# A row tile's partial products: three matmuls of 256 columns in place of one of 512 and one of 256, with packed operand rows

## The chip, the cores and the metric

The kernel runs on one core of a Trainium2 chip. The metric is the device time of one execution in microseconds. Matrix products run on TensorE (PE; PEld is its loading of the stationary operand), elementwise work on VectorE (DVE), ScalarE (ACT) and GpSimd (POOL), and the weights are brought in by transfers that SyncE (SP) issues.

## The reference, cut to what matters

One layer of a hybrid decoder on 256 tokens with 16 learned tokens ahead of them, width 2048, all in float32:

```python
def hybrid_mixer(xn, ...):
    proj = xn @ w_in
    (fq, fk, fv, ff, gq, gk, gv, gr, ga, gate_fox, gate_gla) = jnp.split(proj, split_points, axis=-1)
    o_fox = forgetting_attention(fq, fk, fv, ff, b_forget)        # 8 heads of 128
    ...
    o_gla = gated_linear_attention(gq, gk, gv, g_log)             # 4 heads, keys 256, values 512
    o_gla = (head_rmsnorm(o_gla, gla_norm_g) * jax.nn.silu(gr)).astype(xn.dtype)
    y = jax.nn.sigmoid(gate_fox) * (o_fox @ w_o_fox) + jax.nn.sigmoid(gate_gla) * (o_gla @ w_o_gla)
    return y @ w_out

def squared_relu_mlp(xn, w1, w2):
    return jnp.square(jax.nn.relu(xn @ w1)) @ w2

h = h + hybrid_mixer(rmsnorm(h, norm_mix_g[l]), ...)
h = h + squared_relu_mlp(rmsnorm(h, norm_mlp_g[l]), w_ff1[l], w_ff2[l])      # 2048 -> 8192 -> 2048
return rmsnorm(h, final_norm_g)[:, N_META:]
```

The weights, some 290 MB, are read once.

## The kernel before

Activations lie transposed: 128 features on the partitions, tokens along the row. Every float32 operand is split in two parts that TensorE takes in its rounded float32 form, `hi` and the remainder `lo`, and a product is made of three partial products: hi·hi, hi·lo and lo·hi. The weights are cut into 128-column blocks of 2048 rows (`stream()` lists them in order). `weight_half` loads half a block (128 x 1024, L118), ScalarE makes `whi` of it (L120) and VectorE `wlo` (L121); five buffers of each rotate.

`gemm2` multiplies one weight block with an operand of 256 tokens. It runs over 16 row tiles `k` (8 for the fox output projection). Per row tile `mac2` issues two matmuls: `hi` with the whole operand row of 512 columns (256 columns of hi, then 256 of lo) into a whole PSUM bank (L136), and `lo` with the 256 hi columns into the bank's first half (L137). So the first half of the bank collects hi·hi + lo·hi, and the second half hi·lo. Whoever takes the result out adds the halves: `total` copies the second half to SBUF on ScalarE (L168) and adds it on VectorE (L171), and `add_residual` does so with one more addition (L858 to L860). Three banks of the pool `pg` rotate.

Where the 16 learned tokens are needed too (keys and values of both branches), `gemm_all` issues three matmuls of 272 columns per row tile instead (L153 to L155) and `join` mends the first 16 columns.

The first seven blocks are multiplied while the input still arrives, two row tiles at a time, by `products` (L345, L350; one block with 272 columns at L347, L348 and L352). The last four blocks of the MLP (`ends`) go in two parts: lo·hi for 256 tokens (L912), then for each half of the tokens one matmul of two pieces of 128 columns, hi·hi and hi·lo (L928).

The operands: `x` (normalised input, rows of 544 words: 272 hi, 272 lo) for the input projection; `of`, `og` (outputs of the branches), `y` (their gated sum), `x2` (input of the MLP) and `a` (its hidden part, four groups `g` of 2048). The last five are made by `operand`, which gives each row tile 544 words, with 16 unused ahead of the 512 and 16 behind.

Order: GLA heads, fox heads, then per two output blocks four gates (`gate`), the fox and the GLA output projection; then the projection `w_out`, and per group 16 blocks of `w_ff1` and 16 of `w_ff2`. A scheduler orders each engine's instructions at build time; `later(n, fn)` puts a piece of work behind the n-th gemm from here, so that small matmuls stand between large ones. `gate` takes its bank with `total` and multiplies by the norm on POOL (L816).

Of the kernel before, what the change touches and what calls it, by code (L numbers as in the profile page):

```python
# [7 lines left out]
F32 = mybir.dt.float32  # L8
F32R = mybir.dt.float32r
# [3 lines left out]
ALU = mybir.AluOpType  # L13
# [3 lines left out]
P = 128  # L17
# [3 lines left out]
NT = 256  # L21
NA = NM + NT
EPS = 1e-6
FOX_H, FOX_D = 8, 128
# [41 lines left out]
def trunk(ctx: ExitStack, tc: tile.TileContext, hT, w_small, w_all, consts, w_alpha2, out):  # L66
    nc = tc.nc
    serial = [0]

    def nm(s):  # L70
        serial[0] += 1
        return f"{s}_{serial[0]}"

    const = ctx.enter_context(tc.tile_pool(name="const", bufs=1))
    keep = ctx.enter_context(tc.tile_pool(name="keep", bufs=1))
    wp = ctx.enter_context(tc.tile_pool(name="wp", bufs=5))
    tmp = ctx.enter_context(tc.tile_pool(name="tmp", bufs=2))
    dram = ctx.enter_context(tc.tile_pool(name="dram", bufs=1, space=bass.MemoryType.DRAM))
    pg = ctx.enter_context(tc.tile_pool(name="pg", bufs=3, space=PSUM))
# [4 lines left out]
    def bank(pool, s):  # L84
        return pool.tile([P, 512], F32, tag="bank", name=nm(s))
# [47 lines left out]
        return lambda k: (parts[k // HK][0][:, k % HK, :], parts[k // HK][1][:, k % HK, :])  # L133

    def mac2(ps, hi, lo, x, first, last):
        nc.tensor.matmul(ps, hi, x, start=first, stop=False)  # L136
        nc.tensor.matmul(ps[:, 0:NT], lo, x[:, 0, :], start=False, stop=last)  # L137

    def gemm2(w, x, k0=0, nk=KT):

        ps = bank(pg, "ps")
        for k in range(nk):
            hi, lo = w(k0 + k)
            mac2(ps, hi, lo, x[:, k], k == 0, k == nk - 1)
        issued()
        return ps
# [15 lines left out]
        nc.scalar.copy(b, ps[:, NA : NA + NM])  # L162
        nc.vector.tensor_tensor(ps[:, 0:NM], ps[:, 0:NM], b, op=ALU.add)

    def total(ps, t=None):

        b = tmp.tile([P, NT], F32, tag="evb", name=nm("evb"))
        nc.scalar.copy(b, ps[:, NT:512])  # L168
        if t is None:
            t = tmp.tile([P, NT], F32, tag="evt", name=nm("evt"), bufs=4)  # L170
        nc.vector.tensor_tensor(t, ps[:, 0:NT], b, op=ALU.add)  # L171
        return t

    def split_to(dst_hi, dst_lo, src):
# [42 lines left out]

    def operand(pool, name, nk=KT, at=0, **kw):


        row = 2 * NT + 32
        t = pool.tile([P, at + nk * row], F32R, name=nm(name), **kw)
        t = t[:, at:].rearrange("p (k r) -> p k r", r=row)
        return t[:, :, 16 : 16 + 2 * NT].rearrange("p k (o t) -> p k o t", t=NT)


    h = keep.tile([P, KT, NA + 3], F32, name="h")
# [88 lines left out]
    for s in range(KT // 2):  # L316
        if s + 3 < KT // 2:
            with tc.issue_after(load_stage(s + 3, 0).ins):
                load_h(nc.sync, 2 * s + 6, 2)
            last = load_stage(s + 3, 1).ins  # L320
        wa, wb = stages[s]
        for kk in range(2):
            k = 2 * s + kk
            nc.scalar.activation(x_hi[:, k], h[:, k, 0:NA], AF.Identity, scale=gain(0, k))
            nc.vector.scalar_tensor_tensor(x_lo[:, k, 0:NT], h[:, k, NM:NA], gain(0, k),
                                           x_hi[:, k, NM:].bitcast(F32), op0=ALU.mult, op1=ALU.subtract)
            xm = meta[:, k, :]
# [12 lines left out]

        def products(c, k, part):
            hi, lo = at[c][0][:, k % 2, :], at[c][1][:, k % 2, :]
            ps, st, sp = first_ps[c], k == 0, k == KT - 1
            if part == 0 and c < NF - 1:
                nc.tensor.matmul(ps, hi, x[:, k], start=st, stop=False)  # L345
            elif part == 0:
                nc.tensor.matmul(ps[:, 0:NA], hi, x_hi[:, k], start=st, stop=False)  # L347
                nc.tensor.matmul(ps[:, X_LO], hi, x_lo[:, k], start=False, stop=sp, skip_group_check=True)  # L348
            elif c < NF - 1:
                nc.tensor.matmul(ps[:, 0:NT], lo, x[:, k, 0], start=False, stop=sp)  # L350
            else:
                nc.tensor.matmul(ps[:, 0:NA], lo, x_hi[:, k], start=False, stop=sp)  # L352

        if s < KT // 2 - 1:
            groups = [range(4), range(4, NF)] if s else [range(2), range(2, 4), range(4, NF)]
            order = [(c, 2 * s + kk, part) for g in groups for kk in range(2) for part in range(2) for c in g]
        else:
            order = [(c, 2 * s + kk, part) for c in range(NF) for kk in range(2) for part in range(2)]  # L360
        for o in order:
            products(*o)
        if s in (3, 5, 6, 7):
            with tc.issue_after(copied):
                square((3, 5, 6, 7).index(s))
# [90 lines left out]
    og_box = []  # L456

    def og_tile():
        if not og_box:
            og_box.append(operand(keep, "og", tag="s2"))  # L460
        return og_box[0]

    def gla_gates(ts):
        sg = att.tile([P, 4, NT], F32, tag="sg", name=nm("sg"))
        for i in range(4):
            t = ts[i] if ts else total(gemm2(next_weights(), x))
            nc.vector.tensor_tensor(t, t, rbt, op=ALU.mult)
# [26 lines left out]
    def gla_head(hd, sg, ready=None):  # L494
# [25 lines left out]
            for i in range(2):  # L520
                keys(i, gemm_all(next_weights()))
        for i in range(2):
            t = ready[0][:, i, :] if ready else total(gemm2(next_weights(), x))
# [118 lines left out]
    att = cum.enter_context(tc.tile_pool(name="att", bufs=1, reuse_waits="tile"))  # L642

    join(first_ps[NF - 1])
    ts = [total(ps) for ps in first_ps[0:4]]
    qd0 = att.tile([P, 4, NT], F32, tag="so", name=nm("qd"))[:, 0:2, :]
    for i in range(2):
        total(first_ps[4 + i], qd0[:, i, :])
    ps = bank(pg, "psa")
    for k in range(KT):  # L650
        if k == HK:
# [53 lines left out]
    def fox_head(hd):  # L705
# [106 lines left out]


    def gate():
        t = total(gemm2(next_weights(), x))
# [10 lines left out]
    for j0 in range(0, KT, 2):  # L826
        gates = ahead if j0 == 0 else [gate() for _ in range(4)]
        w = next_weights()
        for j in range(2):
            t = total(gemm2(w, of, k0=8 * j, nk=8))  # L830
            nc.vector.tensor_tensor(gates[2 * j], gates[2 * j], t, op=ALU.mult)
        for j in range(2):
            t = total(gemm2(next_weights(), og))
            nc.vector.tensor_tensor(t, gates[2 * j + 1], t, op=ALU.mult)
# [8 lines left out]


    ht = h[:, :, NM:NA]
    x2 = operand(keep, "x2", tag="s2")

    def square_sum(j, acc):
        if j == 0:
# [4 lines left out]
            nc.gpsimd.tensor_tensor(acc, acc, sq, op=ALU.add)  # L854

    def add_residual(j, ps):
        b = tmp.tile([P, NT], F32, tag="evb", name=nm("evb"))
        nc.scalar.copy(b, ps[:, NT:512])  # L858
        nc.vector.tensor_tensor(ht[:, j, :], ps[:, 0:NT], ht[:, j, :], op=ALU.add)
        nc.vector.tensor_tensor(ht[:, j, :], ht[:, j, :], b, op=ALU.add)  # L860

    acc2 = gat.tile([P, NT], F32, tag="acc", name="acc2", bufs=1)
    for j in range(KT):
# [11 lines left out]


    def relu2(a, f, ps):
        t = total(ps)
        nc.vector.scalar_tensor_tensor(t, t, 0.0, r2b, op0=ALU.max, op1=ALU.mult)
        s = gat.tile([P, NT], F32, tag="asq", name=nm("asq"))  # L880
        nc.vector.tensor_tensor(s, t, t, op=ALU.mult)
        split_to(a[:, f, 0, :], a[:, f, 1, :], s)

    acc = gat.tile([P, NT], F32, tag="acc", name="acc3", bufs=1)
    for g in range(NG):
        a = operand(keep, "a", tag="s1")
        held = []
        for f in range(KT):
            ps = gemm2(next_weights(), x2)
# [169 lines left out]
```

## Time and profile before

| | us |
|---|---|
| median of 3 runs | 1596.99 |
| lowest and highest run | 1596.72, 1597.74 |
| span of the profiled execution, first to last instruction | 1595.0 |
| PE busy in it | 1585.0 |
| DVE busy | 1060.4 |
| ACT busy | 790.8 |
| POOL busy | 125.2 |

The profile is of one execution, whose span is 1595.0 us; what of an execution lies outside the span is read as the median less the span, 2.0 us. In the rows, `L136` is a line of the kernel, `ps<-x,whi` are the tiles written and read, `128x512` is partitions by columns, and of matmuls the durations overlap: the time that one takes from the next is the distance of their starts.

### The profile page before, as it was taken

Reading aid. Unit: us, or ns where it says so; the run is one execution under the profiler, and the core shown is the slowest. Engines: PE = TensorE matmul, PEld = TensorE weight load, DVE = VectorE, ACT = ScalarE, POOL = GpSimd, SP = SyncE. Lnnn points to the kernel's source line nnn. Section 1 sums busy time; section 2 is a strip of 40 time slices with the busy share of each in tenths; the row PEclk is TensorE's granted clock in tenths of the full one; section 3 lists DMA queues with packets and bytes.
Section 4 is the critical chain, followed back from the end, with each engine's and each line's share of the span. In section 5 each row is a group of like instructions: output and inputs, shape, how many; then the busy total and the mean of one; then the engine's idle time right before and its main releaser. Section 6 shows DMA issues by size and latency. Waiting matters only on the chain.

```text
span 1595.0 us, 25427 instructions
## 1 busy us (share of the span) xinstructions
PE 1585.0 (99%) x9812; PEld 1428.8 (90%) x9812; DVE 1060.4 (66%) x1659; ACT 790.8 (50%) x1271; POOL 125.2 (8%) x213
## 2 busy tenths in 40 slices
PE   9999999999999999999999999999999999999997
PEld 8999999999998888888888888888888888888887
DVE  7897757676655555555777776567655776567655
ACT  6665444454455444444555544444444444444563
POOL 6011000011100000000011000000000000000022
PEclk9999999999999999999999999999999999999999
DMA  9444545454445555555555555555555555555552
GB/s 323 156 164 155 180 157 183 167 188 164 159 167 181 191 186 189 189 191 187 186 195 186 188 193 187 188 191 190 187 190 190 186 189 193 186 188 193 186 183 97
DMA packets 86602, 293.09 MB, mean 184 GB/s; under 512 B 9112, under 2 KB 16800, under 8 KB 86352
## 3 DMA queue, kind: packets, MB, share of 16 engines
q1 hardware_dynamic: 85872, 289.62, 53.8%
q8 instruction: 77, 1.26, 0.3%
q0 software_dynamic: 176, 1.12, 0.2%
q10 hardware_dynamic: 432, 0.72, 0.1%
q14 instruction: 45, 0.37, 0.1%
HBM read 289.32 MB, written 2.11 MB: 183 GB/s over the span
## 4 chain that ended last, share of the span: by engine, by line
PE 99%; DMA 0%; issue 0%; POOL 0%; ACT 0%; DVE 0%; SPq 0%; POOLq 0%; ACTq 0%
PE ps L136 51%; PE ps L137 27%; PE psa L155 5%; PE psa L154 5%; PE psa L153 5%; PE ps L345 1%; PE ps L350 1%; PE ps L928 1%; PE pa L548 1%; PE ps L912 0%; DMA raw<-w_all_dram 0%; PE po L611 0%; POOL o L976 0%; PE po L188 0%; PE ps L348 0%
## 5 line engine op out<-in xcount | busy, mean ns | idle before, releaser
L121 DVE TENSOR_TENSOR wlo<-raw,whi 128x1024 fp32r<-128x1024 f32 x522 | 641.0, 1228 | 452.8 <-ACT whi L120 449.4
L120 ACT CAST whi<-raw 128x1024 fp32r<-128x1024 f32 x522 | 548.1, 1050 | 660.0 <-PE ps L136 493.1
L136 PE MATMUL ps<-x,whi 128*128 128x512 f32 x1952 | 683.8, 393 | 0.0
L137 PE MATMUL ps<-x,wlo 128*128 128x256 f32 x1952 | 548.5, 281 | 0.0
L136 PEld LDWEIGHTS ps<-x,whi 128*128 128x128 f32 x1952 | 366.1, 188 | 80.4
L137 PEld LDWEIGHTS ps<-x,wlo 128*128 128x128 f32 x1952 | 368.3, 189 | 0.1
L136 PE MATMUL ps<-a,whi 128*128 128x512 f32 x960 | 334.3, 392 | 0.0
L137 PE MATMUL ps<-a,wlo 128*128 128x256 f32 x960 | 269.1, 281 | 0.0
L136 PEld LDWEIGHTS ps<-a,whi 128*128 128x128 f32 x960 | 179.8, 188 | 39.9
L137 PEld LDWEIGHTS ps<-a,wlo 128*128 128x128 f32 x960 | 181.1, 189 | 0.3
L153 PE MATMUL psa<-x,whi 128*128 128x272 f32 x624 | 181.2, 290 | 0.0
L155 PE MATMUL psa<-x,whi 128*128 128x272 f32 x624 | 181.1, 290 | 0.0
L154 PE MATMUL psa<-x,wlo 128*128 128x272 f32 x624 | 179.4, 288 | 0.0
L153 PEld LDWEIGHTS psa<-x,whi 128*128 128x128 f32 x624 | 118.1, 189 | 0.4
L154 PEld LDWEIGHTS psa<-x,wlo 128*128 128x128 f32 x624 | 117.4, 188 | 0.0
L155 PEld LDWEIGHTS psa<-x,whi 128*128 128x128 f32 x624 | 117.2, 188 | 0.0
L136 PE MATMUL ps<-og,whi 128*128 128x512 f32 x256 | 89.6, 392 | 0.0
L136 PE MATMUL ps<-y,whi 128*128 128x512 f32 x256 | 89.1, 392 | 0.0
L854 POOL TENSOR_TENSOR acc<-acc,hsq 128x256 f32<-128x256 f32 x26 | 28.5, 1097 | 769.2 <-ACT hsq L853 769.2
L137 PE MATMUL ps<-og,wlo 128*128 128x256 f32 x256 | 71.9, 281 | 0.0
L137 PE MATMUL ps<-y,wlo 128*128 128x256 f32 x256 | 71.8, 281 | 0.0
L171 DVE TENSOR_TENSOR evt<-ps,evb 128x256 f32<-128x256 f32 x158 | 65.9, 418 | 0.5 <-ACT evb L168 0.5
(301 smaller groups left out, 1437.0 us busy)
## 6 DMA issues: line engine op xcount, KB each, us to landing
raw<-w_all_dram SPq DMA_DIRECT2D x537, 512.0 KB, 3.6
raw<-w_all_dram SPq DMA_DIRECT2D x8, 384.0 KB, 6.6
h<-hT_dram SPq DMA_DIRECT2D x8, 275.0 KB, 6.7
negc<-fdram POOLq DMA_DIRECT2D x1, 1088.0 KB, 8.0
out_dram<-o SPq DMA_DIRECT2D x2, 512.0 KB, 2.7
raw<-w_all_dram SPq DMA_DIRECT2D x2, 256.0 KB, 3.9
room<-w_small_dram SPq DMA_DIRECT2D x1, 320.0 KB, 7.4
out_dram<-o ACTq DMA_DIRECT2D x1, 320.0 KB, 3.1
```

Source lines behind the costliest of these rows:

```text
L120: nc.scalar.copy(hi[:, k, :], r)
L121: nc.vector.tensor_tensor(lo[:, k, :], r, hi[:, k, :].bitcast(F32), op=ALU.subtract)
L136: nc.tensor.matmul(ps, hi, x, start=first, stop=False)
L137: nc.tensor.matmul(ps[:, 0:NT], lo, x[:, 0, :], start=False, stop=last)
L153: nc.tensor.matmul(ps[:, 0:NA], hi, x_hi[:, k], start=(k == 0), stop=False)
L154: nc.tensor.matmul(ps[:, 0:NA], lo, x_hi[:, k], start=False, stop=(k == KT - 1))
L155: nc.tensor.matmul(ps[:, X_LO], hi, x_lo[:, k], start=False, stop=(k == KT - 1), skip_group_check=True)
L171: nc.vector.tensor_tensor(t, ps[:, 0:NT], b, op=ALU.add)
L345: nc.tensor.matmul(ps, hi, x[:, k], start=st, stop=False)
L350: nc.tensor.matmul(ps[:, 0:NT], lo, x[:, k, 0], start=False, stop=sp)
L548: nc.tensor.matmul(dst, k[:, a], q[:, a, :], start=(a == 0), stop=(a == 1))
L854: nc.gpsimd.tensor_tensor(acc, acc, sq, op=ALU.add)
```

## The change

`mac2` issues three matmuls of 256 columns per row tile, hi with the row's hi columns, hi with its lo columns, and lo with its hi columns, all adding into the first half of the bank. `products` does the same for its six blocks of 256 tokens. The halves need no addition afterwards: `total` goes, consumers read the bank itself, `kept` copies a finished half bank to SBUF for the first six blocks, and the gate's multiplication moves from POOL to VectorE, since it now reads the bank. `operand` packs its rows: 512 words each with no gap, in a tile of the old size, at an offset `at` that is given for each tile.

```diff
     def mac2(ps, hi, lo, x, first, last):
-        nc.tensor.matmul(ps, hi, x, start=first, stop=False)
-        nc.tensor.matmul(ps[:, 0:NT], lo, x[:, 0, :], start=False, stop=last)
+        nc.tensor.matmul(ps, hi, x[:, 0, :], start=first, stop=False)
+        nc.tensor.matmul(ps, hi, x[:, 1, :], start=False, stop=False)
+        nc.tensor.matmul(ps, lo, x[:, 0, :], start=False, stop=last)
 
     def gemm2(w, x, k0=0, nk=KT):
-        ps = bank(pg, "ps")
+        ps = bank(pg, "ps")[:, 0:NT]
...
-    def total(ps, t=None):
-        b = tmp.tile([P, NT], F32, tag="evb", name=nm("evb"))
-        nc.scalar.copy(b, ps[:, NT:512])
+    def kept(ps, t=None):
         if t is None:
             t = tmp.tile([P, NT], F32, tag="evt", name=nm("evt"), bufs=4)
-        nc.vector.tensor_tensor(t, ps[:, 0:NT], b, op=ALU.add)
+        nc.scalar.copy(t, ps[:, 0:NT])
         return t
...
     def operand(pool, name, nk=KT, at=0, **kw):
-        row = 2 * NT + 32
-        t = pool.tile([P, at + nk * row], F32R, name=nm(name), **kw)
-        t = t[:, at:].rearrange("p (k r) -> p k r", r=row)
-        return t[:, :, 16 : 16 + 2 * NT].rearrange("p k (o t) -> p k o t", t=NT)
+        t = pool.tile([P, nk * (2 * NT + 32)], F32R, name=nm(name), **kw)
+        return t[:, at : at + nk * 2 * NT].rearrange("p (k o t) -> p k o t", o=2, t=NT)
...
             if part == 0 and c < NF - 1:
-                nc.tensor.matmul(ps, hi, x[:, k], start=st, stop=False)
+                nc.tensor.matmul(ps[:, 0:NT], hi, x[:, k, 0], start=st, stop=False)
+                nc.tensor.matmul(ps[:, 0:NT], hi, x[:, k, 1], start=False, stop=False)
...
-            og_box.append(operand(keep, "og", tag="s2"))
+            og_box.append(operand(keep, "og", at=32, tag="s2"))
...
-            t = ts[i] if ts else total(gemm2(next_weights(), x))
-            nc.vector.tensor_tensor(t, t, rbt, op=ALU.mult)
+            ps = ts[i] if ts else gemm2(next_weights(), x)
+            t = ps if ts else tmp.tile([P, NT], F32, tag="evt", name=nm("evt"), bufs=4)
+            nc.vector.tensor_tensor(t, ps, rbt, op=ALU.mult)
...
-    ts = [total(ps) for ps in first_ps[0:4]]
+    ts = [kept(ps) for ps in first_ps[0:4]]
...
-    of = operand(late, "of", FOX_H, 32)
+    of = operand(late, "of", FOX_H, 0)
...
     def gate():
-        t = total(gemm2(next_weights(), x))
-        nc.gpsimd.tensor_tensor(t, t, rbt, op=ALU.mult)
+        t = tmp.tile([P, NT], F32, tag="evt", name=nm("evt"), bufs=4)
+        nc.vector.tensor_tensor(t, gemm2(next_weights(), x), rbt, op=ALU.mult)
...
-            t = total(gemm2(w, of, k0=8 * j, nk=8))
+            t = gemm2(w, of, k0=8 * j, nk=8)
...
-    y = operand(keep, "y", tag="s1")
+    y = operand(keep, "y", at=16, tag="s1")
...
-    x2 = operand(keep, "x2", tag="s2")
+    x2 = operand(keep, "x2", at=32, tag="s2")
...
     def add_residual(j, ps):
-        b = tmp.tile([P, NT], F32, tag="evb", name=nm("evb"))
-        nc.scalar.copy(b, ps[:, NT:512])
-        nc.vector.tensor_tensor(ht[:, j, :], ps[:, 0:NT], ht[:, j, :], op=ALU.add)
-        nc.vector.tensor_tensor(ht[:, j, :], ht[:, j, :], b, op=ALU.add)
+        nc.vector.tensor_tensor(ht[:, j, :], ps, ht[:, j, :], op=ALU.add)
...
     def relu2(a, f, ps):
-        t = total(ps)
-        nc.vector.scalar_tensor_tensor(t, t, 0.0, r2b, op0=ALU.max, op1=ALU.mult)
+        t = tmp.tile([P, NT], F32, tag="evt", name=nm("evt"), bufs=4)
+        nc.vector.scalar_tensor_tensor(t, ps, 0.0, r2b, op0=ALU.max, op1=ALU.mult)
...
-        a = operand(keep, "a", tag="s1")
+        a = operand(keep, "a", at=(32, 0, 24, 48)[g], tag="s1")
```

More of the change, by code (lines that the diff above doesn't have):

```diff
@@ L522, in gla_head @@
         for i in range(2):
-            t = ready[0][:, i, :] if ready else total(gemm2(next_weights(), x))
+            t = ready[0][:, i, :] if ready else gemm2(next_weights(), x)
             for q, n, at in ((0, Q1, 0), (Q1, Q3, NT)):
@@ L644, in trunk @@
     join(first_ps[NF - 1])
-    ts = [total(ps) for ps in first_ps[0:4]]
+    ts = [kept(ps) for ps in first_ps[0:4]]
     qd0 = att.tile([P, 4, NT], F32, tag="so", name=nm("qd"))[:, 0:2, :]
     for i in range(2):
-        total(first_ps[4 + i], qd0[:, i, :])
+        kept(first_ps[4 + i], qd0[:, i, :])
     ps = bank(pg, "psa")
@@ L709, in fox_head @@
         nc.vector.tensor_tensor(fk, ps[:, 0:NA], rb, op=ALU.mult)
-        t = total(gemm2(next_weights(), x))
+        t = gemm2(next_weights(), x)
         nc.vector.scalar_tensor_tensor(fq, t, FOX_D ** -0.5, rbt, op0=ALU.mult, op1=ALU.mult)
@@ L814, in gate @@
     def gate():
-        t = total(gemm2(next_weights(), x))
-        nc.gpsimd.tensor_tensor(t, t, rbt, op=ALU.mult)
+        t = tmp.tile([P, NT], F32, tag="evt", name=nm("evt"), bufs=4)
+        nc.vector.tensor_tensor(t, gemm2(next_weights(), x), rbt, op=ALU.mult)
         s = late.tile([P, NT], F32, tag="gate", name=nm("gate"), bufs=6)
@@ L829, in trunk @@
         for j in range(2):
-            t = total(gemm2(w, of, k0=8 * j, nk=8))
+            t = gemm2(w, of, k0=8 * j, nk=8)
             nc.vector.tensor_tensor(gates[2 * j], gates[2 * j], t, op=ALU.mult)
         for j in range(2):
-            t = total(gemm2(next_weights(), og))
-            nc.vector.tensor_tensor(t, gates[2 * j + 1], t, op=ALU.mult)
+            t = tmp.tile([P, NT], F32, tag="evt", name=nm("evt"), bufs=4)
+            nc.vector.tensor_tensor(t, gates[2 * j + 1], gemm2(next_weights(), og), op=ALU.mult)
             nc.vector.tensor_tensor(yf[:, j0 + j, :], gates[2 * j], t, op=ALU.add)
-    y = operand(keep, "y", tag="s1")
+    y = operand(keep, "y", at=16, tag="s1")
     for j in range(KT):
@@ L877, in relu2 @@
     def relu2(a, f, ps):
-        t = total(ps)
-        nc.vector.scalar_tensor_tensor(t, t, 0.0, r2b, op0=ALU.max, op1=ALU.mult)
+        t = tmp.tile([P, NT], F32, tag="evt", name=nm("evt"), bufs=4)
+        nc.vector.scalar_tensor_tensor(t, ps, 0.0, r2b, op0=ALU.max, op1=ALU.mult)
         s = gat.tile([P, NT], F32, tag="asq", name=nm("asq"))
```

## The prediction

> **What bounds the kernel now.** I read the page's busy shares first, then who waited for whom on TensorE, then the chain that ended last.
>
> ```profile
> span 1595.0 us, 25427 instructions
> PE 1585.0 (99%) x9812; PEld 1428.8 (90%) x9812; DVE 1060.4 (66%) x1659; ACT 790.8 (50%) x1271; POOL 125.2 (8%) x213
> PEclk9999999999999999999999999999999999999999
> ```
>
> PE (TensorE matmul) is busy 99% of the span at a granted clock in the top tenth of every slice; VectorE (DVE) is busy 66%, ScalarE (ACT) 50%. Busy matmul time can hide small stalls, so the waits of PE come next: engine, line, what it waited for, total us, times, longest.
>
> ```profile
> PE warm L311 <- DVE ones L195: 1.3, 1, 1.3
> PE pn L952 <- ACT sq L933: 0.7, 1, 0.7
> PE ps L345 <- ACT whi L280: 0.4, 1, 0.4
> ```
>
> That is the whole list: 2.4 us of waiting in 1595, all at the two ends. No eviction of a bank and no weight half ever holds PE up. The chain of waits agrees, by line:
>
> ```profile
> by line: PE ps L136 50.9%; PE ps L137 26.6%; PE psa L155 5.0%; PE psa L154 4.9%; PE psa L153 4.9%; PE ps L345 1.4%; PE ps L350 0.7%; PE ps L928 0.7%; PE pa L548 0.5%; PE ps L912 0.5%; DMA raw<-w_all_dram 0.3%; PE po L611 0.2%; issue 0.2%; P
> ```
>
> L136 (512 columns) and L137 (256 columns) are 77.5% of it. So the time is the sum of what PE needs from one matmul's start to the next, and an edit counts only by what it does to that sum. The profiled execution has a span of 1595.0 us; the median of the runs is 1596.99, so 2.0 us lie outside the span. I add the change to the median.
>
> **How many steps change.** The groups by line and shape give the counts (x covers the tiles x and x2):
>
> ```profile
> L136 PE MATMUL ps<-x,whi 128*128 128x512 f32 x1952 | 683.8, 393 | 0.0
> L137 PE MATMUL ps<-x,wlo 128*128 128x256 f32 x1952 | 548.5, 281 | 0.0
> L136 PE MATMUL ps<-a,whi 128*128 128x512 f32 x960 | 334.3, 392 | 0.0
> L136 PE MATMUL ps<-og,whi 128*128 128x512 f32 x256 | 89.6, 392 | 0.0
> L136 PE MATMUL ps<-y,whi 128*128 128x512 f32 x256 | 89.1, 392 | 0.0
> L136 PE MATMUL ps<-of,whi 128*128 128x512 f32 x128 | 45.1, 393 | 0.0
> L345 PE MATMUL ps<-x,whi 128*128 128x512 f32 x96 | 28.7, 398 | 0.4 <-ACT whi L280 0.4
> L136 PEld LDWEIGHTS ps<-x,whi 128*128 128x128 f32 x1952 | 366.1, 188 | 80.4
> ```
>
> 1952 + 960 + 256 + 256 + 128 + 96 = 3648 row steps, each now one matmul of 512 columns and one of 256. After, each is three of 256: the columns stay 768, and 3648 matmuls with as many weight loads are added (9812 become 13460). Nothing on PE is removed.
>
> **What a step costs now.** Mean durations (393 and 281 ns) are no prices, since matmuls overlap. Starts are. In the MLP stage the table of windows shows PE alone with these pairs, and one stretch of the timeline (start, duration) confirms it (window; its length; then busy us and instructions of PE, PEld, DVE, ACT and POOL; clock; DMA):
>
> ```profile
> 830.00:1560.00 730.00, 730.00 (x4194) 642.10 (x4193) 479.36 (x672) 348.30 (x500) 20.65 (x18) 1.00 0.56 189
> ```
> ```profile
> 899.82 0.39 PE L136 MATMUL ps<-x,whi 128*128 128x512 f32 x1
> 900.05 0.28 PE L137 MATMUL ps<-x,wlo 128*128 128x256 f32 x1
> 900.17 0.39 PE L136 MATMUL ps<-x,whi 128*128 128x512 f32 x1
> ...
> 904.00 0.39 PE L136 MATMUL ps<-x,whi 128*128 128x512 f32 x1
> ```
>
> 4194 matmuls are 2097 pairs in 730.0 us: 348.1 ns a pair. Twelve pairs from 899.82 to 904.00: 348.3 ns. I use 348.3.
>
> **What a step will cost.** The new step is three matmuls of 256 columns in a row, each with its own load, adding into the same 256 columns. The kernel has such runs at its end (L912 and L928, from the chain in order of time: start, length, piece), and gemm_all has the same three products at 272 columns:
>
> ```profile
> 1562.51 5.68 PE ps L912 x48
> 1571.96 7.47 PE ps L928 x64
> ```
> ```profile
> 429.84 0.28 PE L153 MATMUL psa<-x,whi 128*128 128x272 f32 x1
> ...
> 432.10 0.29 PE L188 MATMUL pq<-fksh,fqsh 128*128 128x272 f32 x1
> ```
>
> L912: 5.68/48 = 118.3 ns. L928, whose 256 columns come as two pieces of 128: 7.47/64 = 116.7 ns. gemm_all: 18 matmuls in 2.26 us, 125.6 ns at 272 columns; a column costs (348.3 - 2 x 118)/256 = 0.44 ns, so 16 columns fewer give 118.5. I take the mean of the three, 117.8. The step then is 3 x 117.8 = 353.4 ns, 5.1 more than 348.3. Put differently, halving a 512-column matmul costs one more fixed part of some 5 ns. Sum: 3648 x 5.1 = **+18.6 us**. By L928 alone it is 1.8 x 3648 = +6.6; by L912 alone 6.6 x 3648 = +24.1.
>
> The Trainium skill (TensorE: Matmul & The Clock Gate, section Back-to-back issue gap) gives an isolated warm gap of N/2.4 + 2.5 ns. As an estimate from that page a step would go from 215.8 + 109.2 to 3 x 109.2, 2.5 ns more, and the kernel to about 1606 us. This trace shows 117.8 for 256 columns in place of 109.2, so I keep to the rows.
>
> **The evictions: nothing, on either side.** The second half of a bank no longer exists, so its copy and its add go:
>
> ```profile
> L168 ACT COPY evb<-ps 128x256 f32<-128x256 f32 x160 | 58.3, 365 | 1.3 <-DVE evt L171 1.2 <-PE ps L350 0.2
> L858 ACT COPY evb<-ps 128x256 f32<-128x256 f32 x76 | 27.8, 366 | 0.0
> L171 DVE TENSOR_TENSOR evt<-ps,evb 128x256 f32<-128x256 f32 x158 | 65.9, 418 | 0.5 <-ACT evb L168 0.5
> L860 DVE TENSOR_TENSOR h<-h,evb 128x256 f32<-128x256 f32 x76 | 32.4, 426 | 2.5
> L831 DVE TENSOR_TENSOR gate<-gate,evt 128x256 f32<-128x256 f32 x16 | 6.7, 423 | 0.4
> L121 DVE TENSOR_TENSOR wlo<-raw,whi 128x1024 fp32r<-128x1024 f32 x522 | 641.0, 1228 | 452.8 <-ACT whi L120 449.4
> ```
>
> ACT loses 236 copies and keeps 6 of the same size in kept(): 230 x 0.365 = 84 us less. DVE loses the adds (66 us, and two into qd of about 0.4 each) and L860's 32 us; it takes over the 32 gate multiplications from POOL (32 x 0.42 = 13 us, by L831's size): some 85 us less. All of that lies beside PE, which waits for neither engine outside the ends. Gain on the path: at most the 0.4 us of L345's wait. The cover, were the moves a cost, is DVE's idle third; the gate product on DVE stands behind at most two weight subtractions (L121, 1228 ns each), while the next gemm takes 16 x 0.353 = 5.7 us and three banks rotate. A bank is free earlier than before, by one 365 ns copy and its hand-over, so PE gets no new wait; nothing is queued on PE behind anything new. The DMA queue SP and its weight transfers keep their order and size.
>
> **Instructions.** PE's list grows by 7296 entries, and the list is fetched by DMA (packets, MB, share):
>
> ```profile
> q8 instruction: 77, 1.26, 0.3%
> ```
>
> The sustained rate rises from 2 matmuls in 348 ns to 3 in 353. gemm_all and the L912 run already go at one in 118 to 126 ns, and the list of PE's waits holds none for a fetch, so I cost it at 0. The other bound: the list grows by 13460/9812, some 28 packets, and were each to stop PE for 0.4 us like L345's wait, it would be 11 us.
>
> **Packed rows: an unknown of both signs.** A row of hi and lo was 544 words apart from the next, so its start moved by 128 bytes within 512 from row to row; now the distance is 512 words and every row of a tile starts at one place. That the place matters a little is hinted at by the spread of equal matmuls (min/median/max ns):
>
> ```profile
> L137 PE MATMUL ps<-og,wlo x256: 277/281/284, 495.1 to 781.7; 128*128 128x256 f32 x128
> L912 PE MATMUL ps<-a,wlo x64: 276/280/283, 1562.3 to 1571.7; 128*128 128x256 f32 x64
> ```
>
> The bounds are -4 and +3 ns a matmul around the median, for og, y, of, x2 and a (256 + 256 + 128 + 1024 + 960 = 2624 steps); x keeps its layout (1024 steps with the first 96). I take 0, the median, as the tiles get different places; for the range I allow 0.5 ns, 3 x 0.5 x 2624 = 3.9 us either way.
>
> Forecast: 1597.0 + 18.6 = **1615.6 us**.
>
> **Rivals.**
> *Columns alone count (no change).* If two halves cost what a whole costs, the step stays 348.3 and the time 1597, or 1596.6 with L345's wait gone. For it: L928 at 116.7 is only 0.6 ns above a third of 348.3. Against: L912 and gemm_all, two of three rows. Chance 0.06.
>
> *The packed place is a cheap one (faster).* If every packed row reads at the cheap end, 117.8 - 4 = 113.8 ns, a step of og, y, of, x2 and a takes 341.4, 6.9 less than now: 2624 x -6.9 = -18.1; x's 1024 steps still pay 5.1, +5.2. Time 1597 - 12.9 = 1584. It decides from a mean below 348.3/3 = 116.1 ns in the packed tiles, less the share that x costs: 115.4. For it: some 256-column matmuls do end 4 ns early. Against: the places differ from tile to tile, and the whole spread would have to fall on one side. Chance 0.08.
>
> *The weight load becomes the bound (much slower).* A load shows 188 ns; PEld's 1428.8 us over 9812 loads are 145.6 ns each. If a step could not go below three of these, 436.8 ns, it would add 88.5 x 3648 = 323 us: 1920. The Trainium skill (Perfetto Trace Analysis, section Identifying the Most-Contended Engine) judges TensorE's headroom by the load's busy share, and speaks against adding loads. Against it here: L912 sustains a load every 118.3 ns for 48 in a row, so loads overlap each other. Chance 0.02.
>
> That the change does less than it says, for instance one load serving both products of hi, would change nothing: loads lie under matmuls.
>
> **How the numbers follow.** Forecast 0.84, the three rivals 0.06, 0.08 and 0.02. Range: from +6.6 - 3.9 = 2.7 to +24.1 + 3.9 = 28.0, so 1600 to 1625 us; it leaves out the faster rival, the heavy load and the no-change case, 0.16 together, and a little of the forecast's own tails. A measurement of this kernel tells about 0.2%, 3.2 us, from no change. The forecast's low corner touches that bound, so: faster 0.08, same 0.07, slower 0.85.
>
> **What would show it.** After: PE still 99% with the same short list of waits; 13460 matmuls and loads; three lines of mac2 with starts 117 to 119 ns apart, 353 ns a step, and 830 to 1560 us holding about 6200 matmuls; DVE and ACT each some 85 us less busy; L168, L858 and L860 gone. Wrong would be: steps at 348 or below (then compare x, whose rows kept their place, with the packed tiles), a list of PE waits longer than a few us, or single gaps between matmuls where the instruction list is fetched.

## The result, and the profile after

| | before | after |
|---|---|---|
| median of the runs, us | 1596.99 | 1619.78 (3 runs, 1619.76 to 1619.92) |
| span of the profiled execution | 1595.0 | 1618.2 |
| matmuls | 9812 | 13460 |
| DVE, ACT, POOL busy | 1060.4, 790.8, 125.2 | 993.1, 731.3, 100.7 |

The changed kernel is slower by 22.8 us, ratio 1.0143 [1.0125, 1.0161]. The forecast was 1615.6 us, range 1600 to 1625. (The runs of three experiments below, e1, e4 and e7, fall in two groups 6 to 26 us apart with the same kernel; both groups are given where that matters.)

The page of after, its busy shares, clock, the instruction fetches and the chain by line:

```profile
span 1618.2 us, 32245 instructions
PE 1607.5 (99%) x13460; PEld 1604.6 (99%) x13460; DVE 993.1 (61%) x1455; ACT 731.3 (45%) x1041; POOL 100.7 (6%) x181
PEclk9999999999999999999999999999999999999999
q8 instruction: 106, 1.74, 0.4%
PE ps L138 26%; PE ps L136 26%; PE ps L137 26%; PE psa L156 5%; PE psa L155 5%; PE psa L154 5%; PE ps L923 1%; PE ps L341 1%; PE ps L342 1%; PE ps L347 1%; PE pa L546 1%; PE ps L907 0%; DMA raw<-w_all_dram 0%; PE po L609 0%; POOL o L971 0%
```

PE is as full as before and at the same clock. The three lines of `mac2` carry 78% of the chain, where the two lines before carried 77.5%. The waits of PE (line, what it waited for, total us, times, longest):

```profile
PE warm L307 <- DVE ones L194: 1.3, 1, 1.3
PE pn L947 <- ACT sq L928: 0.7, 1, 0.7
PE ps L341 <- ACT whi L276: 0.5, 2, 0.4
PE ps L136 <- DVE evt L874: 0.3, 1, 0.3
```

The whole list is 2.8 us against 2.4. One entry is new, 0.3 us at the start of the MLP, where a bank waits for `relu2` on DVE. So no wait explains the 23 us; the price of a matmul does. Windows inside the stages of one operand each show it (window; length; busy us and count of PE, PEld, DVE, ACT, POOL; clock; DMA share; GB/s). The stages are `y`, `x2`, then `a` of groups 1, 2 and 3, and last the stretch that the prediction named:

```profile
793.00:883.00 90.00, 90.00 (x752) 90.00 (x751) 58.09 (x64) 43.82 (x63) 14.02 (x14) 1.00 0.55 184
1067.00:1155.00 88.00, 88.00 (x750) 88.00 (x749) 56.05 (x77) 37.98 (x47) 0.00 (x0) 1.00 0.56 187
1158.00:1246.00 88.00, 88.00 (x749) 88.00 (x748) 45.15 (x48) 32.48 (x31) 0.00 (x0) 1.00 0.57 187
1338.00:1426.00 88.00, 88.00 (x757) 88.00 (x756) 45.83 (x49) 33.31 (x33) 0.00 (x0) 1.00 0.57 190
1518.00:1585.00 67.00, 67.00 (x567) 67.00 (x567) 34.57 (x37) 38.12 (x51) 12.71 (x10) 1.00 0.56 188
830.00:1560.00 730.00, 729.66 (x6192) 729.49 (x6191) 433.01 (x538) 307.43 (x358) 18.23 (x16) 1.00 0.56 187
```

A matmul counts where any part of its 0.28 us lies in the window, so its price is (length + 0.28) / count: 120.05 ns for `y`, 117.7 for `x2`, 117.8, 116.6 and 118.7 for the three groups of `a`. The same code, the same shapes, and 3.5 ns between the cheapest and the dearest. The four gates on `x`, from the timeline (start, duration):

```profile
752.24 0.29 PE L136 MATMUL ps<-x,whi 128*128 128x256 f32 x1
...
775.08 0.28 PE L136 MATMUL ps<-of,whi 128*128 128x256 f32 x1
```

Four gemms of 16 steps are 192 matmuls: 22.84 us / 192 = 118.96 ns, 356.9 a step.

By these prices and the starts in the other tiles, against 348.3 before: `x` 1024 steps x 8.6 (the price of the four gates, taken for all of them) = 8.8 us; `y` 256 x 11.8 = 3.0; `og`, `of`, `x2` and groups 0 and 1 of `a`, 1920 x 5.0 = 9.6; group 2 256 x 1.6 = 0.4; group 3 192 x 7.7 = 1.5. Sum 23.3 us; the span grew by 23.2.

### The profile page after: what moved, and what is told of

The parts are those of the page before. It is cut to its first block, busy times and chain, and to the rows that moved or that the text cites. A ratio compares the mean times of both kernels' runs of the same rounds, so it can differ in the third digit from the quotient of the medians.

```text
span 1618.2 us, 32245 instructions
## 1 busy us (share of the span) xinstructions
PE 1607.5 (99%) x13460; PEld 1604.6 (99%) x13460; DVE 993.1 (61%) x1455; ACT 731.3 (45%) x1041; POOL 100.7 (6%) x181
## 4 chain that ended last, share of the span: by engine, by line
PE 98%; DMA 0%; issue 0%; POOL 0%; DVE 0%; ACT 0%; SPq 0%; POOLq 0%; ACTq 0%
PE ps L138 26%; PE ps L136 26%; PE ps L137 26%; PE psa L156 5%; PE psa L155 5%; PE psa L154 5%; PE ps L923 1%; PE ps L341 1%; PE ps L342 1%; PE ps L347 1%; PE pa L546 1%; PE ps L907 0%; DMA raw<-w_all_dram 0%; PE po L609 0%; POOL o L971 0%
## 5 line engine op out<-in xcount | busy, mean ns | idle before, releaser
L137 PE MATMUL ps<-x,whi 128*128 128x256 f32 x1952 | 548.6, 281 | 0.0
L136 PE MATMUL ps<-x,whi 128*128 128x256 f32 x1952 | 547.9, 281 | 0.3 <-DVE evt L874 0.3
L136 PEld LDWEIGHTS ps<-x,whi 128*128 128x128 f32 x1952 | 368.2, 189 | 0.5 <-issue 0.5
L137 PEld LDWEIGHTS ps<-x,whi 128*128 128x128 f32 x1952 | 367.6, 188 | 0.0
L137 PE MATMUL ps<-a,whi 128*128 128x256 f32 x960 | 268.9, 280 | 0.0
L136 PE MATMUL ps<-a,whi 128*128 128x256 f32 x960 | 268.8, 280 | 0.0
L137 PEld LDWEIGHTS ps<-a,whi 128*128 128x128 f32 x960 | 180.4, 188 | 0.0
L136 PEld LDWEIGHTS ps<-a,whi 128*128 128x128 f32 x960 | 180.2, 188 | 0.0
```

The lines of the kernel that those rows point to most:

```text
L136: nc.tensor.matmul(ps, hi, x[:, 0, :], start=first, stop=False)
L137: nc.tensor.matmul(ps, hi, x[:, 1, :], start=False, stop=False)
```

## The experiments

Four words are used below. The *place* of a tile is the byte at which its rows start, modulo 512 (each partition's memory, by the addresses of the built kernel). The weights `whi` and `wlo` always start at place 128. In after, `og` and `x2` are at place 192, `y` at 128, `of` at 448, and the groups of `a` at 192, 64, 160, 256. In before, rows 2176 bytes apart run through four places in turn, and `x` does so in both. The *distance* is the place of the rows less that of the weights. "Pair" is the step of 512 and 256 columns, "three" the step of 3 x 256. Steps are means over the starts in the trace.

**e1: the changed kernel with the old rows.** Only the packing is undone; the calls lose their `at`, and `of` has 32 again.

```diff
     def operand(pool, name, nk=KT, at=0, **kw):
-        t = pool.tile([P, nk * (2 * NT + 32)], F32R, name=nm(name), **kw)
-        return t[:, at : at + nk * 2 * NT].rearrange("p (k o t) -> p k o t", o=2, t=NT)
+        row = 2 * NT + 32
+        t = pool.tile([P, at + nk * row], F32R, name=nm(name), **kw)
+        t = t[:, at:].rearrange("p (k r) -> p k r", r=row)
+        return t[:, :, 16 : 16 + 2 * NT].rearrange("p k (o t) -> p k o t", t=NT)
```

> The three matmuls of 256 columns as in the changed kernel, but og, y, of, x2 and a keep the old rows of 544 words, so that a row's start moves by 128 bytes within 512 from row to row, as x's does. Theory 'place' (what a 256-column matmul costs depends on where its row starts): these tiles then cost what x costs in the changed kernel, 356.4 ns a step in place of 353.3 (og, x2, of), 360.0 (y) and 350 to 356 (a); total 1597.0 + 3648 x 8.1 ns = 1626.5 us. Rival 'instructions only' (each 256-column matmul has one price, and the tiles differ by what runs beside them): as the changed kernel, 1619.8 us.

Measured: 1624.11 us, ratio 1.0170 [1.0148, 1.0192], two runs at 1620.5 and 1621.1 and two at 1627.1 and 1627.6, the profiled one among the latter. Windows in the stages `y` and `x2`:

```profile
793.00:883.00 90.00, 90.00 (x759) 90.00 (x759) 58.22 (x64) 44.66 (x63) 13.97 (x14) 1.00 0.57 186
1067.00:1155.00 88.00, 88.00 (x743) 88.00 (x742) 55.41 (x77) 37.64 (x46) 0.00 (x0) 1.00 0.57 184
```

118.9 and 118.8 ns: with rotating rows every tile costs about what `x` costs (356.3), 356.5 to 356.7 a step. `y` fell from 360 to 356.7 and `x2` rose from 353.3 to 356.6. The packed place is what makes the tiles differ. No trace shows how the steps lie in the two runs at 1620.5 and 1621.1.

**e2: before, with only the wide matmul halved.** Two matmuls into the two halves of the bank, in `mac2` and in the same way in `products`; rows, evictions and additions of before stay.

```diff
-        nc.tensor.matmul(ps, hi, x, start=first, stop=False)
+        nc.tensor.matmul(ps[:, 0:NT], hi, x[:, 0, :], start=first, stop=False)
+        nc.tensor.matmul(ps[:, NT:], hi, x[:, 1, :], start=False, stop=last, skip_group_check=True)
...
```

> The kernel before with one edit: hi's matmul of 512 columns is two of 256, one into each half of the bank. The halves are still copied and added by ScalarE and VectorE, and the rows are the old ones of 544 words. Theory (evictions lie beside TensorE; only the split costs): the same as the run with old rows and no additions, 1626.5 us within 1 us. Rival (removing 230 copies and 200 additions gave something back, or adding into one half bank three times in a row costs something): it differs from that run by more than 2 us, upwards for the first, downwards for the second.

Measured: 1625.58 us, ratio 1.0180 [1.0163, 1.0197], between e1's two groups. Its page, and the stage `y`:

```profile
PE 1613.4 (99%) x13460; PEld 1611.0 (99%) x13460; DVE 1059.7 (65%) x1659; ACT 789.6 (49%) x1271; POOL 130.9 (8%) x213
793.00:883.00 90.00, 90.00 (x760) 90.00 (x759) 63.48 (x80) 48.35 (x79) 13.10 (x14) 1.00 0.58 186
```

118.8 ns, as in e1. DVE is busy 66 us more than in e1 (993.2) and ACT 59 us more, and the time is no longer. So the removed evictions are worth nothing here, and three products into one half bank cost what they cost in two halves, to within e1's own scatter of some 3.6 us. With the old rows, halving the matmul is the whole loss: 28.7 us measured, against 3648 x 8.3 ns (356.6 - 348.3) = 30 us by the steps. Each added matmul brings a weight load with it, and no run tells the two apart.

**e3: before, with only the rows packed** (the places of after, the pair of before).

```diff
-        row = 2 * NT + 32
-        t = pool.tile([P, at + nk * row], F32R, name=nm(name), **kw)
...
+        t = pool.tile([P, nk * (2 * NT + 32)], F32R, name=nm(name), **kw)
+        return t[:, at : at + nk * 2 * NT].rearrange("p (k o t) -> p k o t", o=2, t=NT)
...
+og_box.append(operand(keep, "og", at=32, tag="s2"))
+of = operand(late, "of", FOX_H, 0)
+y = operand(keep, "y", at=16, tag="s1")
+x2 = operand(keep, "x2", at=32, tag="s2")
+a = operand(keep, "a", at=(32, 0, 24, 48)[g], tag="s1")
```

> The kernel before with the changed kernel's packed rows, each tile at the same offset as there, and the matmuls of 512 and 256 columns and all evictions as before. Theory 'place': the pair costs one fixed sum in each packed tile, which differs between tiles by some ns within what single rows showed before, 345.9 to 350.8 ns; total 1597 us give or take 6. Rival 'instructions only': 348.3 ns in every tile, 1597.0 us within 1 us.

Measured: 1606.19 us, ratio 1.0058 [1.0043, 1.0073]. The stages `y` and group 2 of `a`:

```profile
795.00:870.00 75.00, 75.00 (x427) 65.08 (x426) 55.24 (x70) 42.14 (x69) 12.70 (x13) 1.00 0.59 193
1320.00:1400.00 80.00, 80.00 (x463) 70.94 (x462) 47.70 (x62) 34.99 (x46) 0.00 (x0) 1.00 0.58 191
```

With a mean duration of 0.33 us a pair is 2 x 75.33 / 427 = 352.8 ns in `y` and 347.0 in group 2. `x`, untouched, stays at 348.2. The expected bound for packing, 345.9 to 350.8, did not hold: most places cost the pair 351 to 353. Packing alone loses 9.2 us with the pair, but wins 1 to 8 us with the three (e1's runs from 1620.5 to 1627.6, against 1619.8). The two halves of the change do not add.

**s1: other places, three per step.**

```diff
-            og_box.append(operand(keep, "og", at=32, tag="s2"))
+            og_box.append(operand(keep, "og", at=72, tag="s2"))
-    of = operand(late, "of", FOX_H, 0)
+    of = operand(late, "of", FOX_H, 12)
-    y = operand(keep, "y", at=16, tag="s1")
+    y = operand(keep, "y", at=88, tag="s1")
-    x2 = operand(keep, "x2", at=32, tag="s2")
+    x2 = operand(keep, "x2", at=64, tag="s2")
-        a = operand(keep, "a", at=(32, 0, 24, 48)[g], tag="s1")
+        a = operand(keep, "a", at=(120, 8, 40, 56)[g], tag="s1")
```

> The changed kernel with other offsets, so that the rows start at these bytes within 512: og 352, y 416, x2 320, of 496, a 32, 96, 224 and 288 for its four groups (changed kernel: og 192, y 128, x2 192, of 448, a 192, 64, 160, 256). Theory 'place': the steps differ by tile by up to 10 ns; 320 is like 64, 192 and 448 (353.3), and the places that lie 32 bytes off a multiple of 64 are like 160 (350). Rival 'instructions only': steps of 353 ns within 1 in all of them, y at 360 as before.

Measured: 1604.93 us. The stages `x2` (place 320) and group 2 of `a` (place 224):

```profile
1060.00:1140.00 80.00, 80.00 (x708) 80.00 (x708) 52.98 (x72) 35.36 (x43) 0.00 (x0) 1.00 0.60 194
1326.00:1412.00 86.00, 86.00 (x719) 86.00 (x719) 43.16 (x46) 31.47 (x30) 0.00 (x0) 1.00 0.56 183
```

113.4 ns and 120.0: 340 and 360 a step, with the same instructions. That places differ held; my guess which ones are cheap did not (320 was expected like 353.3). A place that beats the pair exists.

**e4: all five packed tiles at place 320.** Only the offsets of after differ.

```diff
+og_box.append(operand(keep, "og", at=64, tag="s2"))
+of = operand(late, "of", FOX_H, 96)
+y = operand(keep, "y", at=64, tag="s1")
+x2 = operand(keep, "x2", at=64, tag="s2")
+a = operand(keep, "a", at=(64, 64, 64, 64)[g], tag="s1")
```

> The changed kernel with og, y, x2, of and a all at byte 320 of 512, where x2's step took 340.1 ns in the sweep. Theory 'place': 2624 steps at 340.1 (8.2 under the kernel before) and x's 1024 steps at about 355.5 (7.2 over): 1597 - 21.6 + 7.4 = 1583 us, faster than the kernel before. Rival (340 belongs to the stage or to that one execution and not to the place): steps of 350 to 357 in some of the five tiles, or runs of the same kernel apart by several us; total 1605 to 1625 us.

Measured: 1584.1 to 1584.2 us in three runs and 1610.47 in a fourth; ratio 0.9920 [0.9899, 0.9941] without the fourth. Nearly the whole MLP:

```profile
1060.00:1540.00 480.00, 480.00 (x4238) 480.00 (x4237) 288.99 (x359) 212.92 (x245) 11.27 (x8) 1.00 0.59 193
```

113.3 ns over 4238 matmuls, 340.0 a step in `og`, `y`, `x2` and `a`; `x` 356.2. From one row tile to the next the rows move on by 2048 bytes and the weights by 512, and still every step of `og` takes 340 ns: what is left over from 512 is all that counts here. The fourth run has no trace. It is 26.4 us longer, which is 13.3 ns x 1984, the steps of `x2` and `a`: it fits the MLP at 353.3 instead of 340.0, but that is worked out, not seen.

**e5: the pair at place 320**, to see whether the place is cheap for a column as such (`operand` of e3, offsets of e4).

```diff
+og_box.append(operand(keep, "og", at=64, tag="s2"))
+of = operand(late, "of", FOX_H, 96)
+y = operand(keep, "y", at=64, tag="s1")
+x2 = operand(keep, "x2", at=64, tag="s2")
+a = operand(keep, "a", at=(64, 64, 64, 64)[g], tag="s1")
```

> The kernel before (matmuls of 512 and 256, evictions of both halves) with packed rows, all five tiles at byte 320. Theory 'place, price by column' (at a cheap place 256 columns cost 113.3 ns and 512 twice that, 226.7): 340.0 a step, 2624 x -8.3 = -21.8, 1575 us. Rival 'place is its own for each width': 346 to 353 a step, 1591 to 1609 us.

Measured: 1609.98 us, ratio 1.0082 [1.0066, 1.0098].

```profile
980.00:1540.00 560.00, 560.00 (x3172) 486.39 (x3172) 354.76 (x493) 254.21 (x356) 4.26 (x3) 1.00 0.57 187
```

2 x 560.33 / 3172 = 353.3 ns a pair, the dear end for the pair. So there is no price by column, and a place is good or bad for a sequence of widths. At this one place halving the wide matmul is even a gain: 340.0 a step for the three in e4, 353.3 for the pair here.

**e6: the weights moved, rows as in after.** A gap of 384 bytes ahead of the weights' pool brings the weights to place 0; the rows stay where they were (`of` at 320).

```diff
+    gap = ctx.enter_context(tc.tile_pool(name="gap", bufs=1)).tile([P, 96], F32, name="gap")
+    nc.gpsimd.memset(gap, 0.0)
```

> The changed kernel with 96 unused words ahead of the weight buffers, which moves every weight tile from byte 128 to byte 0 of 512; og and x2 stay at 192, y at 128, a at 192, 64, 160 and 256. Theory 'distance' (what counts is the row's place less the weights' place): og, x2 and a's first group at distance 192, as byte 320 was before, so 340 ns a step. Theory 'absolute place': og and x2 stay at 353.3, y at 360.0.

Measured: 1604.59 us. `y`, group 0 of `a`, `x2`, and group 3:

```profile
793.00:883.00 90.00, 90.00 (x752) 90.00 (x751) 58.08 (x64) 43.77 (x63) 13.99 (x14) 1.00 0.57 185
960.00:1040.00 80.00, 80.00 (x708) 80.00 (x707) 45.18 (x51) 31.60 (x32) 0.00 (x0) 1.00 0.59 195
1060.00:1140.00 80.00, 80.00 (x709) 80.00 (x708) 52.88 (x72) 35.65 (x44) 0.00 (x0) 1.00 0.60 194
1502.00:1569.00 67.00, 67.00 (x560) 67.00 (x559) 34.15 (x36) 37.59 (x51) 12.74 (x10) 1.00 0.59 187
```

`x2` and group 0 of `a`, at place 192 as in after, go from 353.3 to 340 (113.2 and 113.4 ns); group 3 goes to 120.1. None of these rows moved, so this favours the distance between rows and weights as what counts, 192 here as in e4. Group 2 fits too: at distance 160 it takes 352.0, as group 3 did at that distance in s1, from another place. Two tiles speak against it: `og`, also at distance 192, stayed at 353.2, and `y` takes 360 at distance 128, where group 3 in after took 356. And the gap moved the raw buffers and all pools behind the weights as well, so the weights are not shown to be the cause by themselves.

**s2: other places for the pair** (`operand` of e3; `og`, `of`, `y`, `x2` at 352, 496, 480, 384, groups of `a` at 288, 304, 336, 0).

```diff
+og_box.append(operand(keep, "og", at=72, tag="s2"))
+of = operand(late, "of", FOX_H, 12)
+y = operand(keep, "y", at=104, tag="s1")
+x2 = operand(keep, "x2", at=80, tag="s2")
+a = operand(keep, "a", at=(56, 60, 68, 112)[g], tag="s1")
```

> The kernel before with packed rows at other bytes within 512: og 352, y 480, x2 384, of 496, a 288, 304, 336 and 0. Theory 'place': one sum for each tile, between 340 and 353 ns. Rival 'instructions only': 348.3 in each.

Measured: 1606.13 us; group 0 of `a`, distance 160:

```profile
970.00:1045.00 75.00, 75.00 (x435) 66.04 (x434) 43.31 (x55) 32.14 (x41) 0.00 (x0) 1.00 0.58 190
```

2 x 75.33 / 435 = 346.3 (by the starts 346.8); the others between 350.0 and 353.3. For the pair the best places tried are at distances 160 and 32, 1.6 ns under the rotating rows.

**e7: `x` at place 320 too**, its rows 640 words apart, the other five as in e4; a raw buffer is given up for the room.

```diff
-RAW = 5
+RAW = 4
-    x_row = keep.tile([P, KT, 2 * NA], F32R, tag="s1", name="x")
+    x_row = keep.tile([P, KT * 640], F32R, tag="s1", name="x")
+    x_row = x_row.rearrange("p (k r) -> p k r", r=640)[:, :, 48 : 48 + 2 * NA]
...
```

> The changed kernel with og, y, x2, of and a at byte 320, and x's rows 640 words apart instead of 544, so that x's tokens start at byte 320 too in every row; the memory for it comes from one raw weight buffer (four instead of five). Theory 'distance' (a row 192 bytes past the weights' place costs 113.3 ns per 256 columns): x's 1024 steps fall from 356.2 to 340.0, 16.6 us under the run with x's old rows: 1567.5 us, and the 272-column matmuls settle on one price too, somewhere within 5 us either way. Rival (the fourth raw buffer was needed): TensorE waits for weights, above all in the first 80 us, by several us or more; 1570 to 1585.

Measured: three runs at 1587.6 to 1588.2 us (ratio 0.9942 [0.9925, 0.9959]) and three at 1613.3 to 1614.1. The expected 1567.5 did not come. In the profiled run, of the first group, `y` and `x2`:

```profile
790.00:870.00 80.00, 80.00 (x681) 80.00 (x680) 52.03 (x56) 40.35 (x57) 12.96 (x13) 1.00 0.58 187
1060.00:1140.00 80.00, 80.00 (x708) 80.00 (x707) 53.29 (x73) 35.30 (x43) 0.00 (x0) 1.00 0.60 195
```

`x2` at 113.4 ns, `y` at 117.9, both at distance 192 in one execution, and `og` and `of` at 353.3 a step like `y`; `x` came to 350.5, a mixture: of 893 steps 183 take 339 to 343 ns and 688 take 350 to 355. PE's waits stay short (0.9 us in `products`, the longest but for the start), so the missing buffer is not the reason. Distance 192 has two steps, 340.0 and 353.3, and an execution can have both. One switch can be watched, inside `x2`, at the wait for a bank early in the MLP (two windows, and between them the timeline's line of that wait):

```profile
884.10:894.20 10.10, 10.10 (x88) 10.10 (x88) 8.82 (x16) 3.32 (x4) 0.00 (x0) 1.00 0.60 195
895.14 0.36 PE L136 MATMUL ps<-x,whi 128*128 128x256 f32 x1 [0.35 <-DVE evt L875]
896.00:930.00 34.00, 34.00 (x302) 34.00 (x301) 23.95 (x35) 15.72 (x21) 0.00 (x0) 1.00 0.61 194
```

118.0 ns a matmul before the pause of 0.35 us and 113.5 after it, in the same tile at the same place. In `x` the step goes back and forth between the two values, each time within two steps of other matmuls that come between. So place and distance do not fix the step here by themselves; an interruption of the stream on PE can set it anew, and in this trace nothing else does. What decides for one or the other stays open.

**e8: the pair at its best place**, 288 (distance 160), in all five tiles (`operand` of e3).

```diff
+og_box.append(operand(keep, "og", at=56, tag="s2"))
+of = operand(late, "of", FOX_H, 88)
+y = operand(keep, "y", at=56, tag="s1")
+x2 = operand(keep, "x2", at=56, tag="s2")
+a = operand(keep, "a", at=(56, 56, 56, 56)[g], tag="s1")
```

> The kernel before with packed rows, all five tiles at byte 288, the cheapest place that the pair of 512 and 256 columns showed (346.8 ns in one tile). Theory 'distance': 346.8 in all five, 2624 x -1.5 = -4.0, 1593 us, and x as before at 348.3. Rival (the price belongs to that tile or execution): sums of 350 to 353, 1601 to 1610 us.

Measured: 1592.78 us, ratio 0.9974 [0.9965, 0.9984], all eight runs within 1592.4 to 1593.2.

```profile
980.00:1540.00 560.00, 560.00 (x3232) 492.94 (x3231) 360.26 (x500) 260.12 (x365) 8.45 (x6) 1.00 0.58 190
```

346.7 ns a pair, as expected: so packed rows alone can win 4.2 us too, with before's matmuls.

**s3: how sharp the cheap place is** (three per step; distances 176, 208, 368, 384 for `og`, `y`, `x2`, `of`; 184, 200, 400, 216 for `a`).

```diff
+og_box.append(operand(keep, "og", at=60, tag="s2"))
+of = operand(late, "of", FOX_H, 16)
+y = operand(keep, "y", at=68, tag="s1")
+x2 = operand(keep, "x2", at=108, tag="s2")
+a = operand(keep, "a", at=(62, 66, 116, 70)[g], tag="s1")
```

> The changed kernel with the rows at distances from the weights' place that were not tried, most of them near 192: og 176, y 208, x2 368, of 384, a 184, 200, 400 and 216 bytes. Theory 'distance, exact': 340.0 ns only at 192 and where the last sweep hinted at it (368, 342.5 in of), 350 to 360 at the others. Theory 'two lockings': the cheap step of 340.0 is one of two ways in which loads and streams can lock at many distances (at 192 the MLP stage ran at 340.0 in one part of the executions and, by the total, at 353.3 in the other), so 340.0 is seen at some of the near distances too.

Measured: 1614.83 us; groups 0 and 1 of `a` with `x2` between them:

```profile
970.00:1050.00 80.00, 80.00 (x670) 80.00 (x669) 41.11 (x45) 29.74 (x29) 0.00 (x0) 1.00 0.56 185
1066.00:1150.00 84.00, 84.00 (x744) 84.00 (x743) 55.79 (x76) 37.42 (x47) 0.00 (x0) 1.00 0.60 193
1153.00:1243.00 90.00, 90.00 (x752) 90.00 (x752) 45.34 (x49) 33.03 (x33) 0.00 (x0) 1.00 0.57 185
```

Eight bytes to either side of 192 a step costs 360 (119.8 and 120.1 ns), among the dearest; 368 is a second place at 340 (113.3).

**e9: all five at distance 368** (place 496).

```diff
+og_box.append(operand(keep, "og", at=108, tag="s2"))
+of = operand(late, "of", FOX_H, 12)
+y = operand(keep, "y", at=108, tag="s1")
+x2 = operand(keep, "x2", at=108, tag="s2")
+a = operand(keep, "a", at=(108, 108, 108, 108)[g], tag="s1")
```

> The changed kernel with og, y, x2, of and a all at byte 496, 368 bytes from the weights' place, where x2's step took 340.2 ns in the sweep; x's rows are the old ones. Theory 'distance': 340.0 in the five tiles and 356.3 in x, 1584 us as at byte 320, in every run. Theory 'two lockings': part of the runs, or some of the tiles, at 350 to 356 a step, so runs some 26 us apart or a total between 1590 and 1612 us.

Measured: 1584.43 us (five runs, 1584.12 to 1584.57), ratio 0.9920 [0.9906, 0.9934]. This version beats both kernels in every run. Its page, a wait, and the MLP:

```profile
PE 1572.4 (99%) x13460; PEld 1569.5 (99%) x13460; DVE 993.0 (63%) x1455; ACT 732.0 (46%) x1041; POOL 99.9 (6%) x181
PE ps L136 <- DVE evt L874: 0.5, 1, 0.5
1060.00:1480.00 420.00, 420.00 (x3708) 420.00 (x3707) 256.30 (x324) 178.49 (x200) 0.00 (x0) 1.00 0.60 194
```

113.3 ns. Against after only the places of five tiles differ, and 35 us are gone.

All measured steps of three by distance, packed rows, ns (rotating rows: 356.3 to 356.7):

| distance | 0 | 32 | 64 | 96 | 128 | 160 | 176 | 184 | 192 | 200 | 208 | 216 |
|---|---|---|---|---|---|---|---|---|---|---|---|---|
| step | 360 | 350 | 353 | 360 | 356, 360 | 352 | 358 | 360 | 340, 353 | 360 | 358 | 362 |

| distance | 224 | 256 | 288 | 320 | 368 | 384 | 400 | 416 | 448 | 480 |
|---|---|---|---|---|---|---|---|---|---|---|
| step | 355 | 360 | 353 | 353 | 340 | 356 | 356 | 352 | 353 | 355 |

## Why the prediction was right, and where its terms were off

**The bound** held: PE 99% busy, the same short list of waits, 6192 matmuls where about 6200 were named. An edit counted only by what it did to the starts on PE.

**The step** had the right sign, and halving the wide matmul is what costs: e2 is that edit alone, and it is dearer than forecast, 118.8 ns a matmul with rotating rows, not 117.8, so 8.3 ns a step and not 5.1. But it is not "one more fixed part": that holds as a mean over rotating rows alone. At single places the three cost 7 ns more than the pair (place 128, 360.0 in after against 352.9 in e3) or 13.3 less (place 320, e4 against e5). I had averaged L928 (116.7), whose matmuls are of two pieces, with L912 (118.3) and the 118.5 worked out from `gemm_all`; the latter two, which have the form of the new step, were the nearer. This is the mis-sized term. In `x`, which "still pays 5.1", it comes to 1024 x (8.6 - 5.1) = 3.6 us.

**The packed rows** were taken at 0 with 0.5 ns allowed. The five tiles together cost 14.5 us of the 23.3, where 2624 x 5.1 = 13.4 were forecast, so the mean was near, 1.1 us off. But it is a mean over places between 350 and 360, on tiles that rotating rows would have put at 356.5: the value 0 came out about right because a dearer step and a gain by packing nearly cancel. That is luck, and so in part is the total: with the same instructions, other `at` values gave 1604.9 us (s1), 1614.8 (s3) and 1584.4 (e9), the last outside the forecast's range. The bounds -4 and +3 ns a matmul, read from the spread of L912 and L137, were the better half of that step: 113.3 to 120.6 ns was measured over all places.

**The evictions** at nothing: e2 against e1 shows it to within e1's scatter, and PE's list of waits has none for them but the one below. The work removed was sized well as a sum of durations, and yet the page's busy figures fell by 67 us on DVE and 59 on ACT where some 85 and 84 were named. The groups by line, added up, fall from 1116.7 to 1026.2 us on DVE and from 849.7 to 766.2 on ACT, 90 and 84 us: the page counts the time in which an engine is busy once, also where two of its instructions overlap, and so a removed duration takes less from it. The one new wait, 0.3 us at L874, was not foreseen.

**Instruction fetches** at nothing: 106 packets in place of 77, as estimated, and no wait of PE names one.

**The rivals.** Columns alone count: refuted, e2 is 1.8% slower. The cheap place: not what the change drew, but it is real. Its worked-out price, 113.8 ns and 1584 us, is what e9 measured, 113.3 ns and 1584.43 us, the total by two misses that cancel (the tiles gain 8.3 ns a step where 6.9 were named, and `x` loses 8 where 5.1 were named); what spoke against it, that places differ from tile to tile, was a property of the `at` values alone. The heavy load: refuted in size. PEld is 99% busy in after and 99% in e9, which is 35 us faster with as many loads.

Beside these numbers stand two rules of the Trainium skill. Perfetto Trace Analysis (section Identifying the Most-Contended Engine) judges TensorE's headroom by the load's busy share, beside the share of peak arithmetic: here the load's share is 99% in after and 99% in e9, 35 us apart, so by itself it tells neither that the loads bind nor that there is room. SBUF — State Buffer (section Who interferes with whom) gives TensorE one read port for the moving operand and an independent one for loads: e6 moved the weights, with all pools behind them, and not the rows, and the step of `x2` went from 353.3 to 340. This speaks for an effect of the two on each other in this kernel, by whatever means, but does not prove it.

## What to carry to other kernels

Where PE is full and its waits are few, price an edit by the distance of matmul starts, and take that distance from a row of the very form that will be issued, not from a mean over forms. A change of layout that rides along with a change of instructions has a price of its own: measure each alone, since here they did not add (packing cost 9.2 us with the pair and gave 1 to 8 with the three). Once rows all start at one place, that place is a free parameter, and choosing it by trial was worth 35 us here.

## What the runs showed that I had not expected

- A 256-column matmul with its load costs 113.3 to 120.6 ns by where its rows start within 512 bytes, by all appearances relative to the weights, and 8 bytes aside from the cheapest is among the dearest (distance 192 against 184 and 200). A pair ranges from 346.7 to 353.4, with its best at distances 32 and 160, where the three cost 350 and 352. So whether one wide matmul or two narrow ones are cheaper depends on the place.
- Distance 192 has two steps, 340.0 and 353.3, between runs (e4, by its times) and within one (e7, `x2` against `y`, and `x2` before and after a pause of 0.35 us; e6, `x2` against `og`). Distance 368 gave 340 in `og`, `y`, `x2` and `a` of e9 and in `x2` of s3, with five equal runs; only `of`, whose short gemms stand between others, lay at 342 to 344, in e9 with 93 of 126 steps at 340 and 12 at 353.
- Open: what picks the step at 192 after an interruption, and by what means rows and weights disturb each other, if they do. That their reads collide in memory is the obvious guess, but no run separates it from others. `x` at a fixed place other than 320, and weights with another row length, were not tried.
